# Early writes of the memory rows, paired runs of narrow matmuls, tiles for the cached values, and the order at the start of the FFN, in a one-layer hybrid decoder kernel

## The chip, the core and the metric

The kernel runs on one core of a Trainium2 chip. The time is device microseconds of one execution, and lower is better. The median of three runs of the kernel before is 955.71 us (954.79 to 956.05).

## What is computed

One decoder layer serves a prompt of 512 rows and a sample group of 8 sequences with 4 new rows each (32 rows), with 1024 channels and the same weights, all in float32. The sub-layers, cut to what the change touches:

```
def layer(x, ...):
    h = rms_norm(x, g_mix_pre)
    z = h @ w_in                                  # mLSTM heads and differential-attention heads
    ...
    a = attend(dq, dk, dv, lam)                   # prompt: causal; sample: cached keys and values
    ...
    x = x + rms_norm(mix @ w_out, g_mix_post)
    x = x + rms_norm(mem_attend(rms_norm(x, g_mem_pre), mk, mv, w_mq, w_mo), g_mem_post)
    f, conv_new = conv_ffn(rms_norm(x, g_ffn_pre), conv_buf, w_up, w_dw, b_dw, w_down)
    return x + rms_norm(f, g_ffn_post), ...

def diff_attend(q, k, v, mask, lam):              # two softmaxes per head, subtracted
    s = einsum('bqhcd,bkhcd->bhcqk', q, k) * DA_QK_DIM ** -0.5
    p = softmax(where(mask, s, -inf))
    return einsum('bhqk,bkhd->bqhd', p[:, :, 0] - lam * p[:, :, 1], v)

def mem_kv(mem, g_mem_src, w_mk, w_mv):           # the prompt's 256 memory rows
    mn = rms_norm(mem, g_mem_src)
    return mn @ w_mk, mn @ w_mv
```

The sample group attends to 256 cached positions per sequence (two pages of 128 rows, found through a page table) and, in the cross-attention, to its own cached memory keys and values of 256 rows per sequence.

## The kernel before

Rows are handled in five blocks: 0 to 3 are the prompt's 128 rows each, 4 is the 32 sample rows. A float32 matrix product is made of three products of split operands: a high part (`hi`, a cast on ScalarE) and a low part (`lo`, the source minus the high part, made on VectorE or GpSimd at L147), as weight-hi times x-hi, weight-hi times x-lo, weight-lo times x-hi. ScalarE is ACT in the profile, VectorE DVE, GpSimd POOL, TensorE PE, and SP is the queue that issues most loads.

Weights come through `Weights` (L45): a load into one of six stage tiles (`wst`), then a split into one of four slot tiles (`wslot`, pool `wp`, tag "W"). `W.pump()` emits as many loads as `nslots` allows. `gemmA` (L397) goes block by block with the rows as stationary operand. `gemmB` (L458) has the weights as stationary operand and goes over the rows in two halves, 0 to 255 and 256 to 543; with `half_first` it does the first half of several weight tiles before the second.

The order of each engine's queue is set when the program is built, from the order of the code, priorities, readiness and the pools of tiles. `tc.issue_after(x)` puts instructions behind `x` on its engine, and `burst(t)` does so with high priority, which keeps a run of matmuls together.

The stages and the places that the change touches, in the order of time:

- The memory rows (from the start to about 27 us). The transposed and normed rows (`memT`) are split for `mem_k` (L539), which makes the keys `mk` (evacuation L544, copy of the turned keys L550). The float32 rows are also written to `mem_d` in device memory (L598, four writes of 128 x 512 numbers, issued by ACT) and read back much later for `w_mv`. They are issued behind `evm[1]`, the second evacuation of `mem_k`. Between the steps of `mem_k` the rows of x are normed and turned into `hT`.
- The differential attention (about 245 to 325 us). `prompt` is a pipeline over 16 pairs of block and head: `da_soft` (scores `sda`, softmax `pda`), then `da_turn` (transposes `tpa`, copy `aT` on ACT) and `da_av` (product `oda`). Between its steps the sample group works: `dk_load`, `dk_turn`, `dk_scores` (L1212, `ssc`) over the 8 sequences, then `sample_softmax` (L1056: spread weights `spa`, the copy `spc` on ACT, the turns `spt`, the copies `daz`), then `dv_load` and `dv_out` (L1294, `ops`), whose gathers go through stage tiles. The matmuls of `ssc`, `spa` and `ops` use 32 columns of the array. Behind them the loads of `w_out` follow in SP's queue.
- The cross-attention of the sample group (about 440 to 490 us). `mv_load` (L1446) loads the cached memory values of a sequence, 1 MB each. Sequences 3 to 6 have tiles of the pool of slots, the others two stage tiles each, and 7 is loaded behind the first six runs of `mv_out` (`pso`).
- The second half of the projection `w_mo` and the start of the FFN (about 530 to 565 us). `ev1` (L1139) adds the scaled projection to the rows x (L1152, `xb`), `norm_turn` (L323) turns a block into `fT`, and its scales `rsd` go as a row `rsb` over all partitions (`spread`, L1580), by a matmul and a copy for each block. Then `gemmB` with `half_first` begins, and two more blocks are turned between its tiles (`POS`).

## Time and profile before

| | |
|---|---|
| median of 3 runs | 955.71 us (954.79 to 956.05) |
| profiled execution, whole | 956.55 us |
| profiled execution, span of instructions | 954.8 us |
| granted TensorE clock, mean | 0.997 |
| PE, weight loads, DVE, ACT, POOL busy | 931.0, 808.5, 601.9, 387.8, 196.3 us |
| DMA over the span | 136 GB/s, 130.27 MB |

The profile describes one execution. Busy time is the time in which an engine works on an instruction. A row of the timeline gives start, duration, engine, line, operation, and in brackets how long the engine had stood idle before it and what released it; "x4" joins four such instructions. Engine names with a "q" are issues of DMAs. A wait is put down to the release that came last.

### The profile page before, as it was taken

The page shows a single profiled execution, that of the slowest core. Times are in us where ns is not written, and L with a number is a line of the kernel's source. Part 1 is how long each engine was busy: PE and PEld are TensorE (multiplying, and loading weights), DVE is VectorE, ACT ScalarE, POOL GpSimd, SP SyncE. Part 2 cuts the span into 40 slices and gives each one's busy share as a digit, 9 for nine tenths or more (in the row PEclk, how much of TensorE's full clock was granted, in tenths as well). Part 3 has the DMA queues.
Part 4 walks back from the last instruction along what each step waited for, and adds up shares of the span by engine and source line. Part 5 has one row for each costly group of instructions (what it writes and reads, how often), then busy time and mean ns, then how long its engine had stood idle before and what let it go on. Part 6 is the DMA issues. An engine that isn't in the chain of part 4 may idle for free. (4 is left out here: it accounts for less than half of the span.)

```text
span 954.8 us, 17089 instructions
## 1 busy us (share of the span) xinstructions
PE 931.0 (98%) x6612; PEld 808.5 (85%) x6612; DVE 601.9 (63%) x1130; ACT 387.8 (41%) x750; POOL 196.3 (21%) x384
## 2 busy tenths in 40 slices
PE   8999999999999999999999999999999999999995
PEld 5799787889766778998777799989988997999974
DVE  6745144565886438634654769727758676686767
ACT  6545233344676447624544523332212222222232
POOL 7411000025431217300000444001110110111114
PEclk9999999999999999999999999999999999999998
DMA  8950023344825439855954743063052312512023
GB/s 300 280 171 21 1 89 136 89 124 135 269 86 182 147 102 325 299 166 166 355 215 116 205 133 89 4 177 89 4 144 79 122 26 79 164 48 89 24 92 115
DMA packets 120673, 130.27 MB, mean 136 GB/s; under 512 B 8567, under 2 KB 86232, under 8 KB 120592
## 3 DMA queue, kind: packets, MB, share of 16 engines
q1 hardware_dynamic: 114408, 125.69, 41.5%
q10 hardware_dynamic: 6184, 3.48, 1.2%
q8 instruction: 52, 0.85, 0.4%
q14 instruction: 29, 0.24, 0.1%
HBM read 112.22 MB, written 16.93 MB: 135 GB/s over the span
## 5 line engine op out<-in xcount | busy, mean ns | idle before, releaser
L479 PE MATMUL mm<-fT,wslot 128*128 128x256 f32 x1872 | 236.0, 288 | 0.0
L479 PEld LDWEIGHTS mm<-fT,wslot 128*128 128x128 f32 x1872 | 234.4, 188 | 1.8 <-issue 0.8
L146 ACT CAST wslot<-wst 128x1024 fp32r<-128x1024 f32 x125 | 130.8, 1050 | 257.2 <-PE mm L479 72.4
L147 DVE TENSOR_TENSOR wslot<-wst,wslot 128x1024 fp32r<-128x1024 f32 x125 | 154.2, 1237 | 89.0 <-ACT wslot L146 88.6
L1709 PE MATMUL mm<-wslot,act 128*128 128x512 f32 (+1 forms) x180 | 70.2, 391 | 0.0
L1710 PE MATMUL mm<-wslot,act 128*128 128x512 f32 (+1 forms) x180 | 70.0, 392 | 0.0
L1708 PE MATMUL mm<-wslot,act 128*128 128x512 f32 (+1 forms) x180 | 69.3, 387 | 0.0
L1616 POOL COPY cvo<-u 128x2 f32<-128x2 f32 x43 | 12.1, 281 | 204.3 <-DVE u L1614 194.3
L409 PE MATMUL mm<-wslot,hT 128*128 128x512 f32 x128 | 51.2, 402 | 0.0
L411 PE MATMUL mm<-wslot,hT 128*128 128x512 f32 x128 | 51.0, 400 | 0.0
L479 PE MATMUL mm<-hT,wslot 128*128 128x256 f32 (+1 forms) x384 | 50.9, 289 | 0.0
L410 PE MATMUL mm<-wslot,hT 128*128 128x512 f32 x128 | 50.8, 397 | 0.0
L1611 DVE TENSOR_TENSOR u<-mm,rsb 128x256 f32<-128x256 f32 x43 | 18.2, 425 | 51.2 <-PE mm L479 50.3
L479 PEld LDWEIGHTS mm<-hT,wslot 128*128 128x128 f32 x384 | 49.2, 188 | 0.6 <-issue 0.2
L1708 PEld LDWEIGHTS mm<-wslot,act 128*128 128x128 f32 x180 | 34.3, 191 | 8.0 <-issue 0.8
L1710 PEld LDWEIGHTS mm<-wslot,act 128*128 128x128 f32 x180 | 33.8, 188 | 7.3 <-issue 0.4
L1709 PEld LDWEIGHTS mm<-wslot,act 128*128 128x128 f32 x180 | 33.8, 188 | 7.2
L1628 ACT ACTIVATE c<-c 128x560 f32<-128x560 f32 x21 | 14.1, 671 | 56.7 <-DVE c L1622 56.7
L1622 DVE SCALAR_TENSOR_TENSOR c<-u,cvT,c 128x560 f32<-128x560 f32 x43 | 34.3, 798 | 0.9
L1621 DVE SCALAR_TENSOR_TENSOR c<-u,cvT,c 128x560 f32<-128x560 f32 x43 | 34.1, 793 | 0.2
L1721 DVE TENSOR_TENSOR yp<-mm,yp 128x512 f32<-128x512 f32 (+1 forms) x41 | 27.2, 674 | 5.2 <-PE mm L1710 5.1
L411 PEld LDWEIGHTS mm<-wslot,hT 128*128 128x128 f32 x128 | 24.1, 188 | 5.0
(475 smaller groups left out, 1857.2 us busy)
## 6 DMA issues: line engine op xcount, KB each, us to landing
wst<-in_w_up_dram SPq DMA_DIRECT2D x42, 512.0 KB
wst<-in_w_in_dram SPq DMA_DIRECT2D x28, 512.0 KB
wst<-in_w_down_dram SPq DMA_DIRECT2D x20, 512.0 KB
wst<-in_cache_mem_k_dram SPq DMA_DIRECT2D x16, 512.0 KB
wst<-in_w_mk_dram SPq DMA_DIRECT2D x8, 512.0 KB
xb<-in_x_prompt_dram SPq DMA_DIRECT2D x8, 512.0 KB
wst<-in_cache_dk_dram SPq DMA_DIRECT2D x16, 256.0 KB
wst<-in_cache_dv_dram SPq DMA_DIRECT2D x16, 256.0 KB
```

The costliest lines, as they stand in the source:

```text
L146: nc.scalar.copy(out=hi, in_=src)
L147: (eng or nc.vector).tensor_tensor(out=lo, in0=src, in1=f32(hi), op=SUB)
L409: mm(ps[b], lhsT=xt.hi(k, c0, c0 + n), rhs=s[:, 0, kk, :], start=(k == 0), stop=False)
L410: mm(ps[b], lhsT=xt.hi(k, c0, c0 + n), rhs=s[:, 1, kk, :], start=False, stop=False)
L411: return mm(ps[b], lhsT=xt.lo(k, c0, c0 + n), rhs=s[:, 0, kk, :], start=False, stop=(k == nk - 1))
L479: mm(ps[i], lhsT=s[:, l, k, :], rhs=x(k, c0, c1), start=(k == 0 and j == 0), stop=(k == 7 and j == 2))
L1621: STT(out=c, in0=u[:, 1:EXT - 1], scalar=w[1], in1=c, op0=MUL, op1=ADD)
L1622: STT(out=c, in0=u[:, 0:EXT - 2], scalar=w[0], in1=c, op0=MUL, op1=ADD)
L1708: mm(ps, lhsT=t[:, 0, c0:c0 + P], rhs=s[:, 0, i % 2, cs], start=st, stop=False)
L1709: mm(ps, lhsT=t[:, 0, c0:c0 + P], rhs=s[:, 1, i % 2, cs], start=False, stop=False)
L1710: return mm(ps, lhsT=t[:, 1, c0:c0 + P], rhs=s[:, 0, i % 2, cs], start=False, stop=en)
L1721: VTT(out=y, in0=ps, in1=y, op=ADD)
```

## The change

Seven parts, none of which changes what is computed:

1. The writes of `mem_d` are no longer held behind `evm[1]`.
2. `dk_scores` handles two sequences at a time in one burst.
3. Two steps of the prompt (`step`) stand between the copy `spc` and the turns `spt`, and `spt` is held behind the last `oda` of these steps. The loop over the cached values skips its first two prompt steps.
4. The gathers of cached values go, in pairs of sequences, into tiles of the pool of slots (`vt`), and `dv_out` makes runs of two sequences in bursts, the new rows' product in the last of them. `W.nslots` is 0 in this stage.
5. The cached memory values of sequence 7 get a tile of the pool `sp` and are loaded with those of 3 to 6.
6. `gemmB` with `half_first` takes the x-hi products of channels 0 to 511, of 512 to 1023, and then the x-lo products; a block turned between its tiles is held behind the last matmul.
7. In the `w_mo` projection the addition to x comes in the next block's `mid` (`late`), for block 2 behind the scaling of a turned block; `spread` writes all blocks of a half into one PSUM tile and copies 3 tiles in place of 5.

```
@@ norm_turn
-            VTT(out=tmp, in0=pv, in1=gcol(gname, 4 * q, 4 * q + 4).unsqueeze(2).broadcast_to([P, 4, n]), op=MUL)
+            scaled[0] = VTT(out=tmp, in0=pv, in1=gcol(gname, 4 * q, 4 * q + 4).unsqueeze(2).broadcast_to([P, 4, n]), op=MUL)
@@ gemmB, half_first
-                    for k in range(8):
-                        for j, (l, x) in enumerate(((0, xt.hi), (0, xt.lo), (1, xt.hi))):
-                            mm(ps, lhsT=s[:, l, k, :], rhs=x(k, c0, c1), start=(k == 0 and j == 0), stop=(k == 7 and j == 2))
+                    for k0, l, x in ((0, 0, xt.hi), (0, 1, xt.hi), (4, 0, xt.hi), (4, 1, xt.hi), (0, 0, xt.lo), (4, 0, xt.lo)):
+                        for k in range(k0, k0 + 4):
+                            done[0] = mm(ps, lhsT=s[:, l, k, :], rhs=x(k, c0, c1), start=(k == 0 and l == 0 and x == xt.hi),
+                                         stop=(k == 7 and x == xt.lo))
@@ behind mem_k
-    with tc.issue_after(evm[1].ins):
-        for b in range(2):
-            for q, t in enumerate(kept[b]):
-                nc.scalar.dma_start(out=mem_d[:, 4 * q:4 * q + 4, b * P:b * P + P], in_=t)
+    for b in range(2):
+        for q, t in enumerate(kept[b]):
+            nc.scalar.dma_start(out=mem_d[:, 4 * q:4 * q + 4, b * P:b * P + P], in_=t)
@@ sample_softmax
         nc.scalar.copy(out=a, in_=pa[:, :w])
+        behind = between() if between else None
         pT = at("spt")
-        for g in range(2):
-            tr(pT[:, g * P:(g + 1) * P], a[:, g * P:(g + 1) * P], ident)
+        with tc.issue_after(behind) if behind is not None else nullcontext():
+            for g in range(2):
+                tr(pT[:, g * P:(g + 1) * P], a[:, g * P:(g + 1) * P], ident)
@@ proj_add: ev1 and mid
+            late.append((b, z, rs))
+            if not scale:
+                add(*late.pop(0))
...
         def mid():
-            if len(pend) > LP:
+            if len(pend) > (0 if scale else LP):
                 norm_turn(*pend.pop(0))
+            if late:
+                with tc.issue_after(scaled[0].ins) if late[0][0] == 2 else nullcontext():
+                    add(*late.pop(0))
@@ dk_scores
+        if b % 2 == 0:
+            return
+        for c in (b, b - 1):
+            pair[c] = mmp("ssc")[:, :260]
+            for h in range(H):
+                with burst(t):
+                    t = mm(pair[c][NS * h:NS * h + NS], lhsT=qz[:, h, c // 4].rearrange("p c r -> p (c r)"), rhs=kts[c][:, h, :],
+                           start=True, stop=True).ins
@@ differential attention, the sample group
+    def step():
+        next(prompt)
+        next(prompt)
+        return summed[0].ins
+    aw, az = sample_softmax(sall, su, cv, con("selD"), "da", step)
...
     def dv_load(b):
-        st = vts[b] = stage()
+        if b % 2 == 0:
+            t = wp.tile([P, 2, 1024], F32, name="vt", tag="W")
+            vts[b], vts[b + 1] = t[:, 0], t[:, 1]
@@ dv_out
+        if b % 2 == 0:
+            return
...
+        for c, g in ((b, 1), (b, 0), (b - 1, 0), (b - 1, 1)):
+            for h in range(H):
+                with burst(t):
+                    t = mm(ops[NS * h:NS * h + NS, :P], lhsT=az[g][:, h, c * NS:(c + 1) * NS],
+                           rhs=vts[c][:, g * 512 + h * P:g * 512 + (h + 1) * P], start=(c == 1 and g == 1), stop=False).ins
@@ loop over dv_load and dv_out
-        if t % 2 == 0:
+        if t % 2 == 0 and t > 2:
             next(prompt, None)
@@ mv_load
-        if 2 < b < 7:
-            t = wp.tile([P, 2, DM], F32, name="vt", tag="W")
+        if 2 < b:
+            t = wp.tile([P, 2, DM], F32, name="vt", tag="W") if b < 7 else S([P, 2, DM], F32, "vt")
@@ spread
     def spread(i):
-        while rss and (i or len(rss) > 2):
+        if len(rss) <= (0 if i else 2):
+            return
+        ps = at("rsb")
+        for _ in range(len(rss) - (0 if i else 2)):
             rs, c0, n = rss.pop(0)
-            ps = at("rsb")
-            mm(ps[:, :n], lhsT=rs.broadcast_to([n, P]), rhs=ident[:n, :n], start=True, stop=True)
-            VCP(out=rsb[:, c0:c0 + n], in_=ps[:, :n])
+            c = c0 - HALF[i][0] if c0 < SEQ else 256
+            mm(ps[:, c:c + n], lhsT=rs.broadcast_to([n, P]), rhs=ident[:n, :n], start=True, stop=True)
+        VCP(out=rsb[:, HALF[i][0]:HALF[i][0] + 256], in_=ps[:, :256])
+        if i == 0:
+            VCP(out=rsb[:, SEQ:], in_=ps[:, 256:256 + NS])
@@ ups_of
+                    with tc.issue_after(done[0].ins):
+                        norm_turn(*pend.pop(0))
```

Line numbers of the changed kernel differ from those of before by up to some 50. In the rows below, a name behind `<-` is read and the one ahead of it is written.

The first place is ACT's queue at the start. Before, from the copy of the first turned keys (`mkT`) to the second:

```order
L550 COPY mkT<-mkt 128x512
L544 ACTIVATE mkv<-mm,mrs 128x512
L309 ACTIVATE hN,ssq<-xb 32x1024
L146 CAST wslot<-wst 128x1024
L598 DMA mem_d<-ht 128x4x128
L146 CAST hT_263<-ht 128x4x128
L598 DMA mem_d<-ht 128x4x128
L551 DMA mk_d<-mkT 128x4x128
L545 DMA out_dram<-mkv 128x512
L598 DMA mem_d<-ht 128x4x128 x2
L652 ACTIVATE kT<-mm 128x256
```

Of the changed kernel, ACT's queue from the first cast of `memT` to the last write:

```order
L146 CAST memT_138<-ht 128x4x128
L600 DMA mem_d<-ht 128x4x128
L146 CAST memT_138<-ht 128x4x128
L309 ACTIVATE hN,ssq<-xm 128x1024
L600 DMA mem_d<-ht 128x4x128
L146 CAST memT_138<-ht 128x4x128
L221 CAST wslot<-wst 128x1024
L600 DMA mem_d<-ht 128x4x128
L146 CAST memT_138<-ht 128x4x128
L600 DMA mem_d<-ht 128x4x128
```

The four writes have moved from behind the first `mkT` to between the casts of `memT`, some 20 rows earlier.

The second place is SP's queue at the cached values and `w_out`. Before, the end of the gathers (an ISA row computes an address from the page table, and one stands ahead of each of the 16 gathers):

```order
L1087 DMA wst<-in_cache_dv_dram 128x512
L1087 ISA
L1087 DMA wst<-in_cache_dv_dram 128x512
L231 DMA wst<-in_w_out_dram 128x2x512 x6
L1137 DMA xb<-in_x_sample_dram 32x1024
```

Of the changed kernel, the end of the gathers of keys (`cache_dk`) and the start of those of values:

```order
L1091 DMA wst<-in_cache_dk_dram 128x512
L231 DMA wst<-in_w_out_dram 128x2x512 x5
L1091 ISA
L1091 DMA vt<-in_cache_dv_dram 128x512
L1091 ISA
```

Five loads of `w_out` stand ahead of all the gathers of values, and these write `vt` and no longer stage tiles.

The third place is DVE's queue at the start of the FFN. Before, from the scales of block 1 (`rsd`) to the copies of `rsb`:

```order
L1164 COPY rsd<-rs 128x1
L147 TENSOR_TENSOR wslot<-wst,wslot 128x1024
L332 TENSOR_TENSOR ht<-tp,gT 128x512
L1152 SCALAR_TENSOR_TENSOR xb<-y_5958,rs,xb 128x512
L1152 SCALAR_TENSOR_TENSOR xb<-y_6190,rs,xb 128x512
L147 TENSOR_TENSOR wslot<-wst,wslot 128x1024
L332 TENSOR_TENSOR ht<-tp,gT 128x512
L147 TENSOR_TENSOR wslot<-wst,wslot 128x1024
L1585 COPY rsb<-rsb 128x32
L1585 COPY rsb<-rsb 128x128
```

Of the changed kernel, the same place:

```order
L1174 COPY rsd<-rs 128x1
L147 TENSOR_TENSOR wslot<-wst,wslot 128x1024
L334 TENSOR_TENSOR ht<-tp,gT 128x512
L147 TENSOR_TENSOR wslot<-wst,wslot 128x1024
L334 TENSOR_TENSOR ht<-tp,gT 128x512
L1162 SCALAR_TENSOR_TENSOR xb<-y_5953,rs,xb 128x512
L1162 SCALAR_TENSOR_TENSOR xb<-y_6185,rs,xb 128x512
L147 TENSOR_TENSOR wslot<-wst,wslot 128x1024
L1630 COPY rsb<-rsb 128x256
L1632 COPY rsb<-rsb 128x32
```

The two additions (`xb`) stand behind the second scaling of turned rows (`ht`) and no longer ahead of it, and the copies of `rsb` are two in this place and one for the second half.

More of the change, by code (lines that the diff above doesn't have):

```diff
@@ L1 @@
-from contextlib import ExitStack, contextmanager
+from contextlib import nullcontext, ExitStack, contextmanager
 import concourse.bass as bass
@@ L321 @@
     turned = [None]
+    scaled = [None]
     def norm_turn(h, n, gname, xt, c0, pool=(True, False)):
@@ L456, in gemmA @@
             yield 0
+    done = [None]
     def gemmB(xt, evacs, half_first=False):
@@ L536 @@
     W.pump()
-    evm = []
     def mem_k():
@@ L543, in ev @@
                 t = Z("mkv")
-                evm.append(nc.scalar.mul(out=t, in_=ps, mul=mrs[:, b:b + 1]))
+                nc.scalar.mul(out=t, in_=ps, mul=mrs[:, b:b + 1])
                 nc.scalar.dma_start(out=dst[b * P:(b + 1) * P, 512 * i:512 * i + 512], in_=t)
@@ L1054, in sample_exp, with sample_softmax @@
         ACT(out=sall[:, b, :], in_=ps, func=AF.Exp, bias=nm[:, b:b + 1], accum_out=su[:, b:b + 1])
-    def sample_softmax(sall, su, coef, sel, oname):
+    def sample_softmax(sall, su, coef, sel, oname, between=None):
         cf = small(NB, "scf")
@@ L1114, in proj_add @@
         g = gbc(gname)
-        y0, s0, xb, pend, ready, target = {}, {}, {}, [], [], []
+        y0, s0, xb, pend, ready, target, late = {}, {}, {}, [], [], [], []
         def ssq(b, y, nm):
@@ L1148, in ev1, with add @@
             rs = rstd(ss, n, 1, None)
+            late.append((b, z, rs))
+            if not scale:
+                add(*late.pop(0))
+        def add(b, z, rs):
+            c0, n = rows(b)
             x = xb[b]
@@ L1173, in second @@
             run(gemmA(xt, 8, [4, 0, 1, 2, 3], ev1, block_major=True, before=before, mid=mid, midk=1 if scale else MIDK))
+            while late:
+                add(*late.pop(0))
             while ready:
@@ L1212, in dk_scores @@
     def dk_scores(b):
-        ps = mmp("ssc")[:, :260]
-        for h in range(H):
-            mm(ps[NS * h:NS * h + NS], lhsT=qz[:, h, b // 4].rearrange("p c r -> p (c r)"), rhs=kts[b][:, h, :],
-               start=True, stop=True)
-        VTT(out=ps[:, 256:260], in0=ps[:, 256:260], in1=con("cm4"), op=ADD)
-        sample_exp(sall, b, ps, nm, su)
+        if b % 2 == 0:
+            return
+        pair = {}
+        t = None
+        for c in (b, b - 1):
[4 more added lines that the diff above has]
+                           start=True, stop=True).ins
+        for c, ps in pair.items():
+            VTT(out=ps[:, 256:260], in0=ps[:, 256:260], in1=con("cm4"), op=ADD)
+            sample_exp(sall, c, ps, nm, su)
     def da_soft(i):
@@ L1247, in da_turn @@
         nc.scalar.copy(out=aTs[i][:, :nk], in_=tp[:, :nk])
+    summed = [None]
     def da_av(i):
@@ L1254, in da_av @@
         for j in range(b + 1):
-            mm(op[:, :P], lhsT=aTs[i][:, j * P:(j + 1) * P], rhs=dvN[:, j, h * P:(h + 1) * P],
-               start=(j == 0), stop=(j == b))
+            summed[0] = mm(op[:, :P], lhsT=aTs[i][:, j * P:(j + 1) * P], rhs=dvN[:, j, h * P:(h + 1) * P],
+                           start=(j == 0), stop=(j == b))
         nc.scalar.mul(out=outs[b][:, h, :], in_=op[:, :P], mul=rcs[i][:, 0:1])
@@ L1264 @@
     STT(out=cv, in0=con("cB"), scalar=nlam, in1=con("cA"), op0=MUL, op1=ADD)
-    W.nslots = 2
+    W.nslots = 0
     prompt = pipe(4 * H, da_soft, lambda i: None, da_turn, da_av, da_end)
@@ L1275 @@
         F.run(2.5)
-    aw, az = sample_softmax(sall, su, cv, con("selD"), "da")
+    def step():
[3 more added lines that the diff above has]
+    aw, az = sample_softmax(sall, su, cv, con("selD"), "da", step)
     F.run(4)
@@ L1289, in dv_load @@
     def dv_load(b):
-        st = vts[b] = stage()
+        if b % 2 == 0:
+            t = wp.tile([P, 2, 1024], F32, name="vt", tag="W")
+            vts[b], vts[b + 1] = t[:, 0], t[:, 1]
         for g in range(2):
-            gather("cache_dv", b, g, st[:, 512 * g:512 * g + 512])
+            gather("cache_dv", b, g, vts[b][:, 512 * g:512 * g + 512])
     def dv_out(b):
-        for g in range(2):
+        if b % 2 == 0:
+            return
+        t = None
+        for c, g in ((b, 1), (b, 0), (b - 1, 0), (b - 1, 1)):
             for h in range(H):
-                mm(ops[NS * h:NS * h + NS, :P], lhsT=az[g][:, h, b * NS:(b + 1) * NS],
-                   rhs=vts[b][:, g * 512 + h * P:g * 512 + (h + 1) * P], start=(b == 0 and g == 0), stop=False)
+                with burst(t):
+                    t = mm(ops[NS * h:NS * h + NS, :P], lhsT=az[g][:, h, c * NS:(c + 1) * NS],
+                           rhs=vts[c][:, g * 512 + h * P:g * 512 + (h + 1) * P], start=(c == 1 and g == 1), stop=False).ins
+        if b == NB - 1:
+            for h in range(H):
+                with burst(t):
+                    t = mm(ops[NS * h:NS * h + NS, :P], lhsT=anew[:, h].rearrange("p b t -> p (b t)"), rhs=dvS[:, h * P:(h + 1) * P],
+                           start=False, stop=True).ins
     for t, _ in enumerate(pipe(NB, dv_load, lambda b: None, dv_out)):
-        if t % 2 == 0:
+        if t % 2 == 0 and t > 2:
             next(prompt, None)
         F.run(2)
-    for h in range(H):
-        mm(ops[NS * h:NS * h + NS, :P], lhsT=anew[:, h].rearrange("p b t -> p (b t)"), rhs=dvS[:, h * P:(h + 1) * P],
-           start=False, stop=True)
     oS = T2([P, P], "daoS")
@@ L1494 @@
             t = mk_scores(b)
-    for b in range(3, 7):
+    for b in range(3, NB):
         mv_load(b)
@@ L1506 @@
     mv_out(VORD[:6])
-    mv_load(7)
     W.pump()
@@ L1663, in ups_of @@
                 if i in POS and pend:
-                    norm_turn(*pend.pop(0))
+                    with tc.issue_after(done[0].ins):
+                        norm_turn(*pend.pop(0))
         for i, j in enumerate(js):
```

## The prediction

> **What bounds the kernel now.** I began with the head of the page: the busy time of each engine, and the granted clock in tenths over 40 slices.

> ```profile
> span 954.8 us, 17089 instructions
> ...
> PE 931.0 (98%) x6612; PEld 808.5 (85%) x6612; DVE 601.9 (63%) x1130; ACT 387.8 (41%) x750; POOL 196.3 (21%) x384
> ...
> PEclk9999999999999999999999999999999999999998
> ```

> TensorE (PE) is busy for 98% of the span and its clock is at full speed throughout, so the kernel is bound by TensorE. The change keeps every matmul. It can therefore gain only where TensorE stands still, or where a matmul becomes cheaper through its neighbour in the queue. 954.8 − 931.0 = 23.8 us are idle, part of them at the two ends of the program, which are not touched. The view of waits, cut to TensorE, names those in between (us in total, times, longest):

> ```profile
> PE mm L467 <- POOL fT L147: 1.8, 2, 1.3
> PE tp L330 <- ACT mkT L550: 1.5, 1, 1.5
> PE pso L1464 <- DMA wst<-in_cache_mem_v_dram: 1.4, 1, 1.4
> ...
> PE oda L1255 <- ACT aT L1247: 1.1, 2, 0.9
> PE tpa L1245 <- DVE pda L1237: 0.7, 1, 0.7
> PE spt L1078 <- ACT spc L1075: 0.7, 1, 0.7
> ...
> PE tpa L1245 <- ACT pda L1233: 0.6, 1, 0.6
> PE sda L1229 <- ACT pda L1233: 0.6, 1, 0.6
> ...
> PE mkt L548 <- ACT mkv L544: 0.4, 1, 0.4
> ```

> These nine rows hold 8.8 us, under 1% of the span. All of them lie at the places that the diff touches, so I went through the four places in the timeline.

> **Place 1, the start: the four writes of mem_d.** The timeline around 45 us (start, duration, queue or engine, line, operation, and in brackets the idle time and its releaser):

> ```profile
> 40.85 0.95 ACTq L598 DMA_DIRECT2D mem_d<-ht  x2
> ...
> 43.59 1.23 ACTq L598 DMA_DIRECT2D mem_d<-ht  x1
> ...
> 44.86 1.44 ACTq L598 DMA_DIRECT2D mem_d<-ht  x1
> ...
> 46.35 0.38 ACT L652 ACTIVATE kT<-mm 128x256 f32<-128x256 f32 x1 [1.85 <-PE mm L467]
> ...
> 46.85 0.59 ACT L550 COPY mkT<-mkt 128x512 f32<-128x512 f32 x1
> ```

> The reader is to see that ScalarE (ACT) spends 43.59 to 46.30 on two issues, that its copies of kT and mkT stand behind them, and that mkT then ends at 47.44, where the transposes of the sample rows had waited 1.5 us. The bracket names the matmul as releaser of the kT copy, but ACT's queue was not free before 46.30. The change moves the four issues to some 8 to 13 us. Both waits of this place go: 1.5 + 0.4 = **1.9 us**.

> What is late next is the start itself, since the writes fall into the first loads. The stretches 3 to 15 us and 15 to 25 us (busy us of each engine, PEclk, DMA share, GB/s), and one cast in the second:

> ```profile
> 3.00:15.00 12.00, 10.49 (x44) 6.25 (x43) 8.70 (x12) 8.65 (x13) 8.18 (x10) 1.00 1.05 378
> 15.00:25.00 10.00, 10.00 (x45) 7.97 (x44) 8.57 (x7) 6.77 (x9) 9.66 (x9) 1.00 0.91 291
> ```

> ```profile
> 21.15 1.05 ACT L221 CAST wslot<-wst 128x1024 fp32r<-128x1024 f32 x1 [0.68 <-DMA wst<-in_w_mk_dram]
> ```

> The DMA engines are full there. The four writes carry 256 KB each (128 x 512 numbers of 4 bytes), so 1.05 MB at 378 GB/s is 2.8 us by which the loads of w_mk and of the rows of x can come later. The second x block is issued behind five small loads too, and ACT's issues stand between its casts of memT. The cost is nothing if the slots are early enough, 2.8 us if TensorE stands still for all of it. For nothing speaks that TensorE was busy 10.00 of 10.00 us in the second stretch although a cast waited 0.68 us for its load. I take a quarter of the upper end, **0.7 us**, the size of that one DMA wait. Place 1 gives 1.9 − 0.7 = 1.2 us.

> [...]

> **Place 2, the differential attention, 248 to 303 us.** First the price of entering a run of matmuls that use 32 columns of the array:

> ```profile
> 261.50 0.65 PE L1215 MATMUL ssc<-kT,qz 128*32 128x260 f32 x8
> ...
> 279.78 1.09 PE L1073 MATMUL spa<-das,csz 128*32 128x260 f32 x16
> ...
> 294.13 1.08 PE L1297 MATMUL ops<-wst,daz 128*32 128x128 f32 x32
> ...
> 298.32 0.64 PE L1297 MATMUL ops<-wst,daz 128*32 128x128 f32 x16
> ```

> Two runs of 8 cost 1.30 us, one of 16 costs 1.09: 0.21 us for an entry. Of 128 columns two runs of 16 cost 1.28 us, one of 32 costs 1.08: 0.20 us. The scores of the cached keys now come in pairs, four runs in place of eight: 4 x 0.21 = 0.8 us. The turns with the cached values (ops) go from five runs to three: 2 x 0.20 = 0.4 us. Together **1.2 us**.

> Then the waits. Two prompt steps stand between the copy spc and its turns spt, which takes the 0.7 us, since the oda, tpa and sda of one step fill several us. The other three in this stretch (oda 1.1, sda 0.6) come from ACT's order. The first ops, ACT and SP, in the timeline:

> ```profile
> 284.60 0.86 PE L1297 MATMUL ops<-wst,daz 128*32 128x128 f32 x22
> ```

> ```profile
> 294.37 1.04 ACT L146 CAST wslot<-wst 128x1024 fp32r<-128x1024 f32 x1 [2.72 <-DMA wst<-in_w_out_dram]
> ```

> ```profile
> 256.83 30.64 SPq L1087 DMA_DIRECT2D wst<-in_cache_dv_dram  x16
> 287.58 11.82 SPq L231 DMA_DIRECT2D wst<-in_w_out_dram  x6
> ```

> ACT waits 2.72 us for a weight of w_out while the copies aT that TensorE needs are queued behind that cast; the weight is late because its load was issued behind sixteen gathers of cached values. Now five loads of w_out go ahead of the gathers, and the casts find their data. So 1.1 + 0.6 + 0.7 = **2.4 us** of waits go. The gathers come behind five loads; five times 512 KB at the 378 GB/s above is some 7 us, and the ops that use them start at 284.60, 28 us behind the first old gather.

> The change adds a wait here. The gathers now fill tiles of the pool of four weight slots, so a cast of w_out cannot start before the ops have read the tile that it takes. Behind the waiting cast stand, on ACT, the copies aT. What TensorE does between one run of ops and the oda that needs the next aT:

> ```profile
> 291.05 0.94 PE L1255 MATMUL oda<-dvN,aT 128*128 128x128 f32 x6
> ...
> 292.15 1.02 PE L1229 MATMUL sda<-dkT,dqT 128*128 128x512 f32 x2
> ...
> 293.07 1.08 PE L1229 MATMUL sda<-dkT,dqz 128*128 128x512 f32 x2
> ```

> With the ops of 1.08 that is 4.1 us; two casts of 1.04 us behind a run of ops take 2.1. The wait is hidden unless ACT is late already; then it costs up to those 2.1 us.

> The two tpa waits (0.7 + 0.6) stay in my sum: pda is made by VectorE (DVE) and ACT, and these are near their own limit in this stretch (third and fourth busy time):

> ```profile
> 248.00:260.00 12.00, 10.87 (x99) 8.16 (x99) 11.08 (x36) 10.69 (x35) 5.48 (x8) 1.00 0.89 287
> 260.00:280.00 20.00, 19.38 (x149) 13.04 (x151) 17.71 (x55) 16.24 (x56) 6.51 (x8) 1.00 0.43 147
> ```

> For the same reason not all of the 3.6 us can be kept: a TensorE that asks earlier meets a DVE that is 92% and 89% busy. What comes back, the new wait included, lies between nothing and 3.6 us; I take **1.0 us**, one cast, because most of this falls behind 280 us and under the 4.1 us. Place 2 gives 2.6 us.

> **Place 3, the cached memory values.** SP and TensorE:

> ```profile
> 475.56 0.81 SPq L1454 DMA_DIRECT2D wst<-in_cache_mem_v_dram  x2
> ...
> 481.60 1.07 PE L1464 MATMUL pso<-wst,caz 128*32 128x256 f32 x16 [1.37 <-DMA wst<-in_cache_mem_v_dram]
> ```

> The load of the last batch row is issued when a stage tile comes free at 475.56, and lands 6 us later. It now has a tile of its own and stands right behind the other loads, whose issue was long before. The whole **1.4 us** go; the w_mo loads behind it move up by one place. Nothing stands against it but one more 1 MB transfer at an earlier time.

> **Place 4, the start of the FFN.** DVE, POOL and TensorE, and an undisturbed pair of the same addition:

> ```profile
> 544.63 2.95 POOL L147 TENSOR_TENSOR fT<-ht,fT 128x512 fp32r<-128x512 f32 x2
> 544.78 3.35 DVE L1152 SCALAR_TENSOR_TENSOR xb<-y,rs,xb 128x512 f32<-128x512 f32 x2
> ...
> 547.63 2.64 PE L467 MATMUL mm<-fT,wslot 128*128 128x256 f32 x20 [1.28 <-POOL fT L147]
> ...
> 554.69 1.41 DVE L1152 SCALAR_TENSOR_TENSOR xb<-y,rs,xb 128x512 f32<-128x512 f32 x2 [0.39 <-POOL rs L304]
> ...
> 562.25 0.94 PE L467 MATMUL mm<-fT,wslot 128*128 128x288 f32 x5 [0.49 <-POOL fT L147]
> ```

> TensorE waits for the low halves of fT that POOL makes. The additions beside them take 3.35 us in place of 1.41. In the old order of a column tile, the second matmul already asks for a low half; in the new one 16 matmuls with high halves come first. At 2.64 / 20 = 0.13 us each that is 2.1 us of cover, more than the 1.28 and the 0.49 us that were waited. The additions stand one scaled block later, and spread copies 3 tiles in place of 5. So **1.8 us** go. What can come back is a wait for the high halves, or for the second block's rows, whose addition and statistics are now later: between 0 and 1.8 us, of which I take 0.4, the size of the smaller old wait. Place 4 gives 1.4 us. Behind 562.25 the order of TensorE is the same and it has no wait in that list.

> **The sum**: 1.2 + 2.6 + 1.4 + 1.4 = 6.6 us. The profiled execution took 956.55 us (span 954.8 and 1.75 around it), so 949.95. The median of the runs, 955.71, lies 0.84 below it: **949.1 us**.

> **The rivals.** *(1) The attention stage is bound by DVE and ACT.* Then all of place 2 turns into other waits for pda. For it speak the 11.08 of 12 us; against it that the waits at 281 to 301 us come from ACT's queue order and not from its load. 6.6 − 2.6 = 4.0 us gained: 951.7. *(2) The writes of mem_d delay the start.* The whole 2.8 us are seen at TensorE, 6.6 − 2.1 = 4.5 us gained: 951.2. For it speaks the DMA share of 1.05, against it the 10.00 us without a pause. [...] *(3) The change doesn't do what it says: the waits only change places.* Both of these, and the waits for fT move to the high halves: 6.6 − 2.6 − 2.1 − 1.4 = 0.5 us gained: 955.2. *(4) Slower.* ACT issues the four writes between the casts of memT, the first operand of TensorE. If each issue there takes the longest time seen, 1.44 us, in the full queues, that is 5.8 us, and with 2.8 us of later loads 8.6 us; if ACT does not catch up, the 1.9 us don't go either. Against the other three places, 2.6 + 1.4 + 1.4 = 5.4 us, that is a loss of 3.2 us: 958.9. It decides from a delay of over 5.4 us at the start. Against it speaks that the shorter issues, the first two, took 0.95 us together.

> **Chances and range.** The forecast has 0.54, rivals (1) and (2) 0.14 each, (3) 0.13, (4) 0.05. About 0.2% (1.9 us) is what a measurement can tell from no change. The first three cases lie under 953.8, so faster has 0.82, same 0.13, slower 0.05. If every cost that I set comes out at nothing, 8.7 us are gained (947.0), and with the two tpa waits as well 10.0 (945.7); the low end is 946.0, just inside. The high end takes in (1) and (2) with some 1.7 us for the two together in part: 953.4. Left out are (3), (4), 0.18.

> **What would show each step.** Place 1: no wait of tp for mkT, writes of mem_d before 15 us, and TensorE busy all through 15 to 25 us; wrong if TensorE waits for wslot or memT there. Place 2: ssc runs of 16 at about 1.1 us, no DMA wait ahead of ACT's casts of w_out, spt without a wait; wrong if tpa or sda wait over 1 us more. Place 3: no wait of pso. Place 4: no wait of mm for POOL, additions near 1.4 us a pair; wrong if a wait for the rsb tiles or for ht stands in its place. The prediction as a whole is wrong if the time of TensorE's last matmul is not some 6 to 7 us earlier, since the tail behind it is untouched.

## The result, and the profile after

The changed kernel takes 949.45 us in the median of six runs (948.55 to 950.86), the kernel before 955.88 us (954.79 to 957.41, six runs): a ratio of 0.9932, with a 95% interval of 0.9918 to 0.9945. That is 6.4 us less. The profiled execution of the changed kernel took 948.76 us.

The head of its page, as for the kernel before:

```profile
span 947.0 us, 17080 instructions
...
PE 927.3 (98%) x6612; PEld 808.2 (85%) x6612; DVE 601.1 (63%) x1128; ACT 388.5 (41%) x750; POOL 195.9 (21%) x384
```

TensorE still has 6612 records and is busy 3.7 us less; the rest of the 7.8 us between the two spans is idle time that is gone. Its view of waits (us in total, times, longest):

```profile
PE mm L413 <- POOL memT L147: 1.6, 2, 1.0
PE tpa L1269 <- DVE pda L1261: 1.4, 2, 1.1
...
PE tp L332 <- DVE hN L318: 1.0, 2, 0.7
PE oda L1281 <- ACT aT L1271: 0.9, 1, 0.9
PE tpk L1225 <- ACT kT L1226: 0.5, 1, 0.5
...
PE mm L472 <- ACT fT L146: 0.3, 1, 0.3
```

Gone are the waits for mkT, for spc, for the DMA of cache_mem_v, for pda ahead of sda, and for POOL's fT. New are the waits for hN at the start, a larger one for memT, two for kT, and an oda that waits 0.9 us for aT at another place than before.

Where the 7.8 us lie is read from the first starts of five groups of matmuls, which stand in the same order in both programs. A row of such a view has the line, engine and operation, the count, the shortest, median and longest duration in ns, and the first and last start. Before:

```profile
L479 PE MATMUL mm<-hT,wslot x384: 276/288/402, 71.3 to 245.9; 128*128 128x256 f32 x192
L1073 PE MATMUL spa<-das,csz x16: 382/382/410, 279.8 to 280.5; 128*32 128x260 f32 x16
L467 PE MATMUL mm<-hqT,wslot x192: 277/289/365, 384.1 to 409.1; 128*128 128x256 f32 x96, 128*128 128x288 f32 x96
L1584 PE MATMUL rsb<-cpk,rsd x10: 271/275/376, 544.9 to 561.0; 128*128 128x128 f32 x8, 32*128 32x32 f32 x2
L479 PE MATMUL mm<-fT,wslot x1872: 276/288/386, 574.6 to 905.3; 128*128 128x256 f32 x186, 128*128 128x288 f32 x2
```

And after:

```profile
L485 PE MATMUL mm<-hT,wslot x384: 274/288/402, 69.8 to 244.5; 128*128 128x256 f32 x192
L1075 PE MATMUL spa<-das,csz x16: 382/382/408, 278.3 to 279.0; 128*32 128x260 f32 x16
L472 PE MATMUL mm<-hqT,wslot x192: 277/292/365, 379.7 to 404.7; 128*128 128x256 f32 x96, 128*128 128x288 f32 x96
L1629 PE MATMUL rsb<-cpk,rsd x10: 271/275/376, 539.1 to 553.4; 128*128 128x128 f32 x8, 32*128 32x32 f32 x2
L485 PE MATMUL mm<-fT,wslot x1872: 276/288/386, 566.7 to 897.3; 128*128 128x256 f32 x186, 128*128 128x288 f32 x2
```

The first row is the plain loop of `gemmB` on hT (its 256-column form), the last the same loop on fT; hqT holds the turned rows from which the queries of the cross-attention are made. The differences of the first starts make stages, and those of every kernel of the experiments are put beside them, from the same rows; all in us:

| kernel | start to long hT product | to spa | spa to hqT | hqT to rsb | rsb to long fT | median (runs) |
|---|---|---|---|---|---|---|
| before | 71.3 | 208.5 | 104.3 | 160.8 | 29.7 | 955.88 (6) |
| changed | 69.8 | 208.5 | 101.4 | 159.4 | 27.6 | 949.45 (6) |
| again (changed) | 67.9 | 208.4 | 101.4 | 159.4 | 27.3 | 949.45 (5) |
| u_mem: writes held | 70.3 | 208.4 | 101.4 | 159.3 | 27.4 | 949.44 (6) |
| held2: the same | 70.7 | 208.4 | 101.4 | 159.8 | 27.6 | 949.94 (5) |
| b_late: held longer | 71.3 | 208.4 | 101.4 | 159.3 | 27.2 | 949.01 (5) |
| u_pair: no pairs | 68.0 | 208.5 | 101.5 | 159.3 | 27.2 | 948.68 (6) |
| u_step: no steps between | 68.6 | 208.5 | 102.7 | 159.5 | 27.5 | 949.44 (5) |
| u_dv: stage tiles | 68.6 | 208.4 | 105.4 | 159.3 | 27.4 | 952.13 (8) |
| u_mv7: late load | 68.6 | 208.5 | 101.4 | 160.9 | 27.3 | 949.60 (5) |
| u_ord: old loop order | 69.2 | 208.5 | 101.4 | 159.4 | 30.8 | 951.09 (5) |
| u_late: early additions | 70.3 | 208.5 | 101.4 | 159.3 | 28.0 | 950.26 (5) |
| b_at: spc behind aT | 68.7 | 208.5 | 101.1 | 159.3 | 27.3 | 947.27 (5) |
| b_best: and memT behind aT | 69.5 | 208.4 | 100.2 | 159.3 | 27.4 | 947.03 (5) |

Two things are to be seen. Four of the five stages repeat within some 0.5 us from one execution to the next where no edit touches them, and often within 0.1, so one profile is enough to price an edit there (u_ord, below, is the exception). The first stage does not: the changed kernel itself shows 69.8 and 67.9 us, and its eleven runs lie between 946.64 and 951.47 us. So the stages, not the medians, decide below. Without the first stage, the change gained 2.9 + 1.4 + 2.1 = 6.4 us, which is the whole difference of the medians.

### The profile page after: what moved, and what is told of

Same layout as the page of the kernel before. It is cut to its first block, busy times and chain, and to the rows that moved or that the text cites. A ratio compares the mean times of both kernels' runs of the same rounds, so it can differ in the third digit from the quotient of the medians.

```text
span 947.0 us, 17080 instructions
## 1 busy us (share of the span) xinstructions
PE 927.3 (98%) x6612; PEld 808.2 (85%) x6612; DVE 601.1 (63%) x1128; ACT 388.5 (41%) x750; POOL 195.9 (21%) x384
## 5 line engine op out<-in xcount | busy, mean ns | idle before, releaser
L146 ACT CAST wslot<-wst 128x1024 fp32r<-128x1024 f32 x125 | 130.8, 1050 | 251.3 <-issue 71.7
L147 DVE TENSOR_TENSOR wslot<-wst,wslot 128x1024 fp32r<-128x1024 f32 x125 | 155.1, 1245 | 81.3 <-ACT wslot L146 80.8
L1770 DVE TENSOR_TENSOR yp<-mm,yp 128x512 f32<-128x512 f32 (+1 forms) x41 | 27.2, 673 | 5.2 <-PE mm L1759 5.1
```

Of the source, the lines that this page charges most:

```text
L146: nc.scalar.copy(out=hi, in_=src)
L147: (eng or nc.vector).tensor_tensor(out=lo, in0=src, in1=f32(hi), op=SUB)
L1770: VTT(out=y, in0=ps, in1=y, op=ADD)
```

## The experiments

**Place 1: the writes of mem_d.** Two kernels hold them as before, in the changed kernel (with `evm` filled by the evacuations of `mem_k`):

```
+    with tc.issue_after(evm[1].ins):
         for b in range(2):
             for q, t in enumerate(kept[b]):
                 nc.scalar.dma_start(out=mem_d[:, 4 * q:4 * q + 4, b * P:b * P + P], in_=t)
```

> The changed kernel with the four writes of mem_d held behind the second evacuation of mem_k again. Theory: the place of the writes makes the gain of the start, so the wait of tp for mkT (1.5 us) returns, the long w_in product (the first matmul of gemmB's plain form on hT) starts near 71.3 us as before and not at 69.8, and the kernel is 1.5 us slower than the changed one (1.0 to 2.0). Rival: the start gains by the hi-first order of the first hT product, not by the writes; then the long product still starts near 69.8 and the time is within 0.5 us of the changed kernel.

> The changed kernel with the writes of mem_d held behind the second evacuation again, a second time. Theory: 0.5 to 1.5 us slower than the changed kernel of this call, with a wait of tp for mkT of 0.6 to 1.5 us in the profile. Rival: within 0.4 us.

The medians are 949.44 and 949.94 us, against 949.45 and again 949.45 us with the early writes:

> The changed kernel itself once more, for its start on the same chip as the next three. From the first plain hT product to the end it should take 869.9 us within 0.4, as in its first profile; what varies between its executions lies ahead of that. Theory: the early writes are worth about 1 us of the start, so over its runs it is 0.5 to 1.5 us faster than the kernel with held writes of this call. Rival: the difference of the first two profiles was chance of the first loads; then the two medians lie within 0.4 us.

So the first expectation fails by time, and the second is met by neither theory clearly: the held writes are 0.5 us slower than the changed kernel that was measured beside them and level with its first measurement, while its single runs spread over 4.8 us. The waits of u_mem show what is exchanged:

```profile
PE oda L1284 <- ACT aT L1274: 0.9, 1, 0.9
PE mm L413 <- POOL memT L147: 0.6, 1, 0.6
PE tp L332 <- ACT mkT L556: 0.6, 1, 0.6
```

The wait for mkT is back with 0.6 us (0.7 in held2) and no longer 1.5, and the 1.0 us for hN are not there; but in `again`, with early writes, they are not there either. In the changed kernel the hN that are late wait for their rows (ACT, timeline):

```profile
22.71 1.06 ACT L309 ACTIVATE hN<-xb 128x1024 f32<-128x1024 f32 x1 [3.85 <-DMA xb<-in_x_prompt_dram]
...
46.09 1.06 ACT L309 ACTIVATE hN<-xb 32x1024 f32<-32x1024 f32 x1 [1.75 <-DMA xb<-in_x_sample_dram]
```

The same hN of the second block ran at 18.39 us before. The reason is in SP's queue, whose order changed as well. Its issue of x blocks before, the issues at the same place after, and SP's longest wait in the first 60 us after:

```profile
8.70 0.94 SPq L581 DMA_DIRECT2D xb<-in_x_prompt_dram  x2
```

```profile
17.93 0.27 SPq L167 DMA_DIRECT2D grow<-in_g_ffn_pre_dram  x1
...
18.98 0.36 SPq L585 DMA_DIRECT2D xb<-in_x_prompt_dram  x1
```

```profile
SPq L167 <- DMA mem_d<-ht: 4.3, 1, 4.3
```

Before, the first two blocks of x were issued together, ahead of five small loads of gains (`grow`). In the changed kernel the second block stands behind these five, and SP stood 4.3 us at one of them, by the profile for a write of mem_d. So the block was issued some 10 us later, and it is this order, more than the time of the transfers, that makes its hN late. All ten profiles with early writes have this wait of SP (2.7 to 4.6 us); the three with held writes do not, and issue the two blocks together. Why a small load waits for that write, the record does not show.

Little of it is seen at TensorE. From 15 to 25 us TensorE is busy for 10.00 of 10.00 us, and its two waits for hN come later, 0.29 us at 38.00 and this one for the sample rows, whose load was issued at 40.31 us and at 32.22 before:

```profile
49.09 0.65 PE L332 MATMUL tp<-cpk,hN 32*128 32x32 f32 x8 [0.72 <-DVE hN L318]
```

A third kernel holds the writes behind `evm[3]`, near 54 us:

> The changed kernel with the four writes held still longer, behind the fourth evacuation of mem_k, some 54 us from the start. Theory: the writes cost the start part of 2.8 us of transfer when they run between 9 and 18 us, as late x rows; at 54 us they cost nothing there and ACT has slack, so it is 0.5 to 1.5 us faster than the changed kernel of this call, with no wait of tp for DVE hN. Rival: the early transfers are hidden and ACT's four issues near 54 us put new waits on kT or mkT; then it is level or up to 1.5 us slower.

It took 949.01 us (948.13 to 949.69), 0.4 us under the changed kernel that was measured beside it, and its first stage is no shorter (71.3 us). It has no wait for hN, as expected, but 2.4 us for POOL's memT and 1.0 us for rows of mem_prompt, which lie ahead of any of the writes and so are not their doing. The start varies from run to run by more than these edits change, so the place of the writes is worth between nothing and about 1 us.

All runs together allow an estimate. The code of the start is the same in all ten kernels with early writes, but for the loop order in u_ord. If a kernel's span behind its first stage is taken from its profile, each of its runs gives a first stage. The median is 69.95 us over the 50 runs of nine kernels with early writes (u_ord is left out), 70.65 over the 16 runs of the three that hold them, and 70.55 over the 39 runs of the kernel before. That is a gain of some 0.6 us, with a standard error of 0.3. The eleven runs of the changed kernel by itself show none of it (70.6).

**Place 2: pairs of scores.** `dk_scores` one sequence at a time, four matmuls each, as before:

> The changed kernel with the scores of the cached keys one sequence at a time. Theory: between 248 and 278 us DVE and ACT set the pace, and the four saved entries of 0.2 us each came back as waits for pda; spa starts at 278.3 us as in the changed kernel (278.0 to 278.7) and the time is within 0.4 us of it. Rival: the entries are saved on the path; then spa starts 0.8 us later, and so does the end.

From the long hT product to spa it takes 208.5 us with pairs, without, and in the kernel before. The four entries are saved and come back. The waits of u_pair against those of the changed kernel say where:

```profile
PE tpa L1261 <- DVE pda L1253: 0.7, 1, 0.7
PE tpa L1261 <- ACT pda L1249: 0.6, 1, 0.6
PE ssc L1231 <- DVE kT L1226: 0.3, 1, 0.3
```

With pairs TensorE waits 1.4 us for pda and 0.5 and 0.3 us for kT, together 2.2; without them 1.6. So 0.6 of the 0.8 us are seen as waits, and the theory that DVE and ACT set the pace there holds.

**Place 2: the steps between spc and spt.** `sample_softmax` without `step`, and all prompt steps in the loop over the cached values:

```
-    aw, az = sample_softmax(sall, su, cv, con("selD"), "da", step)
+    aw, az = sample_softmax(sall, su, cv, con("selD"), "da")
...
-        if t % 2 == 0 and t > 2:
+        if t % 2 == 0:
```

> The changed kernel without the two prompt steps between spc and spt (and with all steps in the loop over the cached values). Theory: the steps removed the wait of spt (0.7 us) but TensorE now waits 0.9 us for the copy aT that stands behind spc on ACT, so undoing them changes nothing: spt waits 0.7 us again, oda waits under 0.2 us at that place, time within 0.4 us of the changed kernel. Rival: the steps are worth their 0.7 us and more, since they also keep the ops fed; then it is 0.7 to 1.5 us slower.

Spa to hqT takes 102.7 in place of 101.4 us, so by this stage the two edits are worth 1.3 us, as the rival said (the median, 949.44 us, is level). Its timeline has the wait of spt, and another one 38 us later:

```profile
278.69 0.44 PE L1082 MATMUL spt<-cpk,spc 128*128 128x128 f32 x2 [0.49 <-ACT spc L1077]
...
317.17 1.16 PE L1281 MATMUL oda<-dvN,aT 128*128 128x128 f32 x8 [0.75 <-ACT aT L1271]
```

The second wait is not one that the steps were meant for: ACT's cast of the memory rows (memT), which waits 2.24 us for its load, stands ahead of that aT. It is most of the 0.8 us that lie behind the first matmul of w_out. Ahead of it the stretch is 0.5 us longer; the waits there are as long as in the changed kernel (spt 0.49 and an oda 0.33, against 0.87), and the ops take four runs in place of three. The rival's reason, that the steps keep the ops fed, is not seen.

The first is the wait that the change set out to cover. In the changed kernel it is covered, but oda waits in its place (TensorE and ACT, timeline):

```profile
278.30 1.09 PE L1075 MATMUL spa<-das,csz 128*32 128x260 f32 x16
280.26 0.94 PE L1281 MATMUL oda<-dvN,aT 128*128 128x128 f32 x6 [0.87 <-ACT aT L1271]
```

```profile
279.45 0.38 ACT L1077 COPY spc<-spa 128x260 f32<-128x260 f32 x1 [0.45 <-PE spa L1075]
279.73 0.48 ACT L1271 COPY aT<-tpa 128x384 f32<-128x384 f32 x1
```

The build set the first of the two steps ahead of spa, so that one step stands behind it; its oda needs an aT whose copy stands behind spc on ACT, and spc waits for spa. The aT was free to go before. A kernel that copies spc behind that aT:

```
+        if between:
+            between()
+        with tc.issue_after(copied[0].ins) if between else nullcontext():
             nc.scalar.copy(out=a, in_=pa[:, :w])
```

(`between` makes one step at each call, and `da_turn` keeps its copy in `copied`.)

> The changed kernel with ACT's copy spc put behind the copy aT of the first of the two steps. Theory: in the changed kernel TensorE waits 0.9 us for that aT only because spc, which waits for spa, is ahead of it in ACT's queue; so the wait goes, spa to w_out takes 21.3 to 21.6 us in place of 22.2, and the time is some 0.7 us less. Rival: ACT and DVE set the pace there and the 0.9 us come back as waits for pda or a later aT; then 22.0 us or more.

The oda starts without a wait, and spa to the first matmul of w_out takes 21.1 us. But spa to hqT falls only by 0.3, to 101.1 us. ACT's timeline shows what stands ahead of the last aT:

```profile
313.28 1.05 ACT L146 CAST memT<-wst 128x1024 fp32r<-128x1024 f32 x1 [2.10 <-DMA wst<-mem_d]
314.24 0.63 ACT L1130 ACTIVATE sqj<-y 32x512 f32<-32x512 f32 x1
...
314.98 0.58 ACT L1276 COPY aT<-tpa 128x512 f32<-128x512 f32 x1
```

The cast of the memory rows, read back from mem_d for w_mv, now stands ahead of that aT and waits 2.10 us for its load. One more line puts it behind:

```
+    with tc.issue_after(copied[0].ins):
         mT = mem_again()
```

> The changed kernel with spc behind the copy aT, and the casts of the memory rows read back from mem_d held behind the last aT. Theory: the last kernel lost 0.7 of its 1.0 us because the cast of memT, which waits for the DMA, stood ahead of an aT on ACT; so spa to w_out takes 21.1 us and from there to the first hqT product 79.2 us, 1.0 us less than the changed kernel in all. Rival: the 0.7 us come from DVE and stay; then 79.9 us in the second stretch.

Spa to hqT is 100.2 us, 1.2 less than in the changed kernel, and no wait of oda is left. Its median is 947.03 us (946.92 to 948.48), a ratio to before of 0.9914 (0.9900 to 0.9927). It beats both kernels by its stage; the 2.4 us between its median and that of the changed kernel measured beside it are more than the stage explains. The rest is put down to the spread of the start, which is not shown.

**Place 2: tiles for the gathers.** `dv_load` with one stage tile for each sequence, and `W.nslots = 2`; the runs of ops stay paired:

> The changed kernel with the gathers of cached values in stage tiles again, one for each sequence, and two slots ahead. From the first spa to the first matmul of w_out the kernel before took 25.1 us and the changed one 22.2. Theory: the place of the w_out loads ahead of the gathers is worth 1.5 to 2 of these 2.9 us, so the stretch takes 23.7 to 24.2 us and ACT's casts of wslot wait for the DMA of w_out again. Rival: runs of ops and the steps ahead of them carry it; then it stays under 22.8 us.

Spa to hqT takes 105.4 us, 4.0 more than in the changed kernel and 1.1 more than before; from spa to w_out it is 25.2. The theory is right in its cause and too small. The edit undoes the tiles, the slots and the order of the loads together: w_out is again issued behind all 16 gathers. Its waits and ACT's timeline:

```profile
PE oda L1281 <- ACT aT L1271: 4.6, 3, 2.9
```

```profile
295.90 1.04 ACT L146 CAST wslot<-wst 128x1024 fp32r<-128x1024 f32 x1 [4.04 <-DMA wst<-in_w_out_dram]
```

ACT waits 4.04 us for a weight of w_out, and the aT behind it hold TensorE. In the changed kernel the casts at that place wait for ops at most:

```profile
288.08 1.98 ACT L146 CAST wslot<-wst 128x1024 fp32r<-128x1024 f32 x2
...
295.91 1.04 ACT L146 CAST wslot<-wst 128x1024 fp32r<-128x1024 f32 x1 [0.40 <-PE ops L1337]
```

**Place 3: the load of sequence 7.** `mv_load(7)` back behind `mv_out(VORD[:6])`, into two stage tiles:

> The changed kernel with the cached memory values of sequence 7 in two stage tiles, loaded behind the first runs of pso. Theory: the wait of pso for that DMA (1.4 us) returns, and from the first pso to the last cpo it takes 23.9 us as before in place of 22.5. Rival: the other loads are earlier now and cover it; then under 22.9 us.

HqT to rsb takes 160.9 us in place of 159.4, and the wait is back:

```profile
PE pso L1506 <- DMA wst<-in_cache_mem_v_dram: 1.6, 1, 1.6
```

The theory holds with 1.5 us.

**Place 4: the order of gemmB's half_first loop.** The old loop (for each of 8 k: hi, lo, hi) in the changed kernel:

> The changed kernel with gemmB's half_first loop in the old order (hi, lo, hi for each of 8 channels blocks). Theory: the order is what covers the low halves at the start of the FFN, so waits of mm for POOL's fT of about 1.8 us return between 540 and 560 us, and the kernel is 1.8 us slower than the changed one (1.2 to 2.4). Rival: the later additions and the single rsb tile cover them; then under 0.5 us slower.

In the profile, rsb to the long fT product takes 30.8 us in place of 27.6: 3.2 us, more than the theory's 1.8 and slower than before (29.7). By the medians it is 1.6 us (951.09 against 949.45), as the theory said. TensorE, and then the windows behind the wait (busy time of PE, PEld, DVE, ACT, POOL, then PEclk, DMA share and GB/s):

```profile
541.91 6.68 PE L472 MATMUL mm<-fT,wslot 128*128 128x256 f32 x42 [1.80 <-POOL fT L147]
```

```profile
541.90:543.50 1.60, 1.59 (x7) 1.59 (x8) 1.60 (x2) 0.09 (x1) 1.43 (x1) 0.50 0.92 261
543.50:545.20 1.70, 1.70 (x10) 1.70 (x9) 1.70 (x3) 1.01 (x2) 0.04 (x1) 0.50 0.35 120
545.20:547.00 1.80, 1.80 (x17) 1.80 (x16) 1.80 (x5) 0.71 (x4) 1.49 (x2) 1.00 0.95 271
```

The wait is 1.80 us as expected, but behind it the granted clock is 0.50 for 3.3 us, in which 17 matmuls run where 17 fit into 1.8 us afterwards. That is the other 1.5 us. They belong to this execution, as far as the mean of the granted clock tells: it is 0.994 here and 0.996 in the four other runs, and 3.4 us at half clock make 0.002 of it. In the changed kernel TensorE goes through without a stop (its rows, and DVE's and POOL's):

```profile
539.93 5.71 PE L472 MATMUL mm<-fT,wslot 128*128 128x256 f32 x46
```

```profile
541.76 2.89 DVE L1162 SCALAR_TENSOR_TENSOR xb<-y,rs,xb 128x512 f32<-128x512 f32 x2
...
542.57 1.53 POOL L147 TENSOR_TENSOR fT<-ht,fT 128x512 fp32r<-128x512 f32 x1 [0.18 <-ACT fT L146]
```

**Place 4: the additions.** `ev1` adds at once again, and `mid` turns a block only when two are pending:

```
-            if not scale:
-                add(*late.pop(0))
+            add(*late.pop(0))
...
-            if len(pend) > (0 if scale else LP):
+            if len(pend) > LP:
```

> The changed kernel with the additions of the w_mo projection made at once in ev1 again, and blocks turned as late as before. From the first rsb to the first matmul of the plain loop on fT the kernel before took 29.7 us, the changed one 27.5, and the one with the old loop order 30.8. Theory: with the new order the low halves have 2 us of cover, so the place of the additions matters little: 27.5 to 28.3 us. Rival: the additions beside POOL's low halves are the cause by themselves; then 28.8 us or more, and waits of mm for fT return.

28.0 us in place of 27.2 to 27.6: the theory's range. The new order carries most of this place, the additions and the earlier turns 0.4 to 0.8 us.

## Why the prediction was right

The time was forecast at 949.1 us and is 949.45. It named as a sign of error that the last matmul is not some 6 to 7 us earlier. In the two profiles it begins at 943.37 and at 935.42 us, 7.95 us earlier; 1.5 us of this are the start of these two executions, which the medians (6.4 us) do not bear out. By its steps:

- **What bounds the kernel** was right: all that was gained are waits and entries of TensorE, and behind the start of the FFN nothing moved.
- **Place 1** was forecast at 1.2 us. It gave nothing to 1 us, 0.6 by the estimate above. The 1.9 us of waits did go. The term that was mis-sized is the cost, 0.7 us, and its reason was incomplete: it was a time of transfer at DMA engines with a share of 1.05 and 0.91, and TensorE was busy throughout the stretch where it was looked for. What the profiles show is SP held for 2.7 to 4.6 us and a load of x behind five small ones. The prediction names this order and gives it no term. The changed profile also has 1.0 us of waits for hN and 1.0 us more for memT, but these change between executions of the same kernel (none and 0.6 in `again`), so they cannot be put down to the writes.
- **Place 2** was forecast at 2.6 us and gave 2.9, partly by other means. The 0.8 us for the pairs were wrong: with DVE 92% and 89% busy in the kernel before, the entries turned into waits for pda and kT, which was put down as a doubt and not as a term. The 0.7 us of spt only moved to oda, as u_step and b_at show. What carries the place is the w_out loads ahead of the gathers, with the tiles that allow it: undone, 4.0 us come back. From spa to w_out it took 25.1 us with 2.4 of waits before, and 22.2 with 0.9 after, so 1.4 us went otherwise, where I had 0.4 for fewer entries. The ops are 0.6 of it (4.7 us busy before, 4.1 after); the rest is not taken apart. The added wait of ACT's casts behind ops was hidden, as forecast: 0.40 us of ACT's time and none of TensorE's.
- **Place 3** was right, 1.4 us forecast, 1.4 measured and 1.5 when undone.
- **Place 4** was forecast at 1.4 us and gave 2.1. The 1.8 us went, and only 0.3 us came back, for ACT's high half. The term was mis-sized because that wait cost more than its idle time: before, four matmuls began at 545.61 us, and at 0.13 us each the fifth was due at 546.13; it began at 547.63, 1.5 us late for an idle time of 1.28. The rest of the 0.7 us is not taken apart. The cover of 16 matmuls was the right reason. That the additions would run in near 1.4 us was wrong: the first pair took 2.89 beside POOL's 1.53, against 3.35 before and 1.41 for the pair of before at 554.69. It is still long; nothing waits for it any more.
- **The rivals.** (1) was right for the first half of place 2 and wrong for the second. (2), that the writes delay the start, came about in part; rows of x came late, and it is seen in hN, but by the order of SP's queue and not with 2.8 us of TensorE's time: the block of x for which ACT stood idle 3.85 us was issued only at 18.98 us, behind SP's wait of 4.3 us. (3) and (4) did not come.

So the bound and the causes of places 3 and 4 were right, but that the sum came within 0.4 us is partly luck: by the stages and medians, 1.2 us too much at the start stood against 0.3 us too little at place 2 and 0.7 at the FFN, and within place 2 the 0.8 us too much for the pairs against some 1 us too little behind them. The range held all runs of the changed kernel.

## What to carry to other kernels

When a wait of the bounding engine is covered by moved work, look on the queue of the engine that releases it for what stands behind the waiting instruction: here spc in front of aT, and casts in front of aT twice, gave or took 0.9 to 4 us each. An instruction that waits for a transfer should stand behind the copies that the bounding engine needs (worth 0.9 us from b_at to b_best). Saved work counts only where the engine beside it has room, which the busy time by stage shows in advance: here DVE was busy for 92% and 89% of its two windows, and the stage up to spa took 208.5 us with pairs and without. When an edit moves DMA issues on one queue, compare the order of the other queues too: here the moved writes of ACT also changed SP's order and held it. And find out which stages repeat before pricing an edit by a time: here four of five repeat within 0.5 us, and the fifth hides 1 us.

## What the runs showed of the hardware

In the profiled execution of u_ord, a wait of TensorE of 1.80 us was followed by a granted clock of 0.50. In that of u_mv7, a wait of 1.6 us made its stage 1.5 us longer and no more, and in that of u_dv, the windows behind a wait of 2.9 us, from 298.8 us on, show a clock of 1.00. So in these three executions the length of a stop did not decide what it cost, and in u_ord the 1.80 us of waiting were followed by a loss of another 1.5. The half clock of u_ord lasts from 541.78 to 545.20 us (same columns as above):

```profile
538.37:541.78 3.41, 1.74 (x11) 1.34 (x10) 3.41 (x4) 2.30 (x4) 3.41 (x3) 1.00 0.55 154
541.78:545.20 3.42, 3.29 (x15) 3.29 (x16) 3.42 (x4) 1.22 (x3) 1.55 (x2) 0.50 0.61 184
```
